# Sparse attention: three low parts on GpSimd, reordered joints, one place for u's high parts, gathered rows four columns later

## The chip, the cores and the metric

The kernel runs on one core of a Trainium2 chip. The metric is the time on the device in microseconds (us) of one execution of the whole program. An execution is also profiled; the profile gives the span from its first to its last instruction, and each engine's instructions. The engines are PE (TensorE, matmuls), DVE (VectorE), ACT (ScalarE), POOL (GpSimd) and SP (SyncE, which here only issues DMAs).

## The reference, cut to what matters

The input is 256 tokens of width 1024 in float32. There are two layers; each has an attention and then an expert network, and after each of the four comes `layer_norm(alpha * h + f(h))`.

- Layer 0's attention is latent attention with 16 heads.
- Layer 1's attention is sparse attention with 16 heads in 4 groups: per head a branch over compressed blocks, one over selected blocks and one over a window, each with a softmax, summed with learned gates. With 256 tokens the selected blocks and the window cover all earlier keys, so the last two branches run over the same causal pairs with keys and values of their own.
- The expert network: queries `h @ w_q` are scored against sub-keys, the 16 best of 128 x 128 experts are taken for each of 8 heads, and the result is the sum over the chosen experts e of `gate * gelu(u[e] . h) * v[e]`.

The kernel computes the expert network for nearly all tokens densely: u of all experts against all tokens, times a matrix of gates that is zero for experts not chosen, and then against all of v.

## The kernel before, in words

**Split matmuls.** All products are of float32 accuracy. Each weight tile (128 rows, 1024 columns) is split into a high part `hi`, which ACT rounds to the fast matmul type (line 125), and a low part `lo = raw - hi`, which DVE computes (line 136). Activations are split in the same way into `hT[0]` and `hT[1]`. A product is then three matmuls: high by high, high by low, low by high.

**The stream of weights.** All weight tiles of the program lie in one list, `stream`, in the order of use (`plan`, line 50). SP loads a tile into one of four places (`_sdma`, line 93), ACT makes its high part (`_shi`, line 113), DVE its low part (`_slo`, line 128), and PE uses both. `nxt` (line 154) hands out the next pair and prepares the ones after it: the low part of one tile and the high part of two tiles ahead. Four high and four low tiles exist at a time, so an engine runs at most a few tiles ahead of PE. `odd` says for a tile which of two offsets (0 or 32 elements) its high part has in its buffer: without an entry always 0, with one the offset alternates with the count `nh`. The four buffers lie 1056 elements apart, that is 16.5 times 64, so with the offset always 0 the tiles start by turns at two places modulo 64 elements, and with the alternating one all at the same place.

**Order.** Instructions run on each engine in the order in which the program writes them; there is no planner. What waits on an engine holds all that is written after it for that engine.

**The expert network** (`peer`, line 449) has a query stage, then 128 u steps (`u_step`, line 727: first narrow ones, and once the choice of experts is done wide ones, in which the high part meets both parts of the activations in one matmul of 512 columns), then 128 v columns (the loop that starts at `rate, gc`). A v column j takes one tile of v: ten matmuls, six for the first token half and four for the second. The 64 last tokens are not computed densely there. For them POOL gathers rows of v (`g_row`, line 476) and the activations of the chosen experts (`g_act`, line 482) by indirect DMA, and DVE multiplies and adds (`g_mac`, line 486, 64 times in column order). `LEAD` and `rate` set the columns in which this happens: gather c comes at column `LEAD + int(rate * c)`, and `rate` makes the last one fall on column 118. The last ten tiles of v are kept for the second token half ("kept tiles", `keep`).

**The joints.** After each attention or expert network comes a layer norm in two token halves (tt) and two column halves (hf): `ln_sum`, `ln_stats`, `ln_mid`, `ln_scale`, and `ln_T` (line 302), in which PE transposes, ACT copies the high part, and a returned function makes the low part on DVE. While the second token half is normalised PE starts on the next stage's first four weight tiles: `early_mm(tt, x, w, tiles)` (line 1229) runs the matmuls of token half tt with part x of the activations and part w of the weights; `early_close` (line 1241) runs all that are left. `ln_last` (line 321) writes out this order. It is called from the end of `peer` and from `out_close` (line 1152), the end of both attentions. Joint A is that after layer 0's attention, B that after layer 0's experts, C that after layer 1's attention.

**The sparse attention's head loop** (`for st in range(NH + 3)`, line 1501) runs one step per head: scores of head st, exponentials, the scaling of the probabilities of the head before (line 1566), transposes of the head two before, products with the values of the head three before. Beside it run, by step, the last two query tiles (steps 0 and 2), the compressed branch (steps 0 to 7, with small products on POOL), and from step 6 on every second step one tile of the output projection. `nxt` in these prepares weight tiles, and so low parts fall into steps 0, 2, 6, 8 and so on.

Of the kernel before, what the change touches and what calls it, by code (L numbers as in the profile page):

```python
# [34 lines left out]
FIRST, NEXT = 44, 10  # L35
GT = 64
ND = S - GT
RING, LEAD = 6, 7
AHEAD = 12
GB = 0.8  # L40
GS = 2.0 ** 15
# [2 lines left out]
class Kern:  # L44
# [5 lines left out]
    def plan(self):  # L50
        I, L = self.I, []
        self.v0s, self.spare, self.pairs = [], None, {}
        self.nh, self.odd = 0, {}
        if "mla" in self.parts:
            L += [I["a_w_in"][k] for k in range(KC)]
            L += [I["a_wk"][i] for i in range(2)]
            L += [I["a_wq"][i] for i in range(3)]
            L += [I["a_wv"][i] for i in range(2)]
            L += [I["a_wq"][i] for i in range(3, 6)]
            L += [I["a_wo"][i] for i in range(KC)]  # L60
        for l in (0, 1):
            if l == 1 and "nsa" in self.parts:
                L += [I["s_wv"][i] for i in range(4)]
                L += [I["s_wT"][i] for i in range(4)]
                L += [I["b_wg"]]
                L += [I["s_wT"][i] for i in range(4, 8)]
                L += [I["b_wq"][i] for i in range(4)]
                L += [I["b_wq"][i] for i in range(4, 8)]
                L += [I["b_wo"][i] for i in range(KC)] + [I["b_wo"][i] for i in range(KC // 2)]
            if f"peer{l}" in self.parts:  # L70
                L += [I["p_wq"][l, i] for i in range(16)]
                L += [I["p_u"][l, (P - FIRST + j) % P] for j in range(P)]
                self.v0s.append(len(L))
                o = (len(L) - self.v0s[0]) % 4
                self.odd.update((len(L) + j, 1) for j in range(P))
                self.pairs.update((len(L) + j, I["p_v"][l, j:j + 2].rearrange("j i d -> i j d")) for j in range(o % 2, P - 1, 2))
                L += [I["p_v"][l, j] for j in range(P)]
        self.stream = L
        self.v0 = self.vb = self.v0s[0]
        self.si = 0  # L80
        self.sd = 0
        self.sh = 0
        self.sl = 0
        self.raws, self.his, self.los = {}, {}, {}
        self.share = False
        self.alt = {}
        self.later, self.now = [], 0

# [39 lines left out]
    def _slo(self, upto, eng=None):  # L128
        while self.sl <= min(upto, len(self.stream) - 1):
            i = self.sl  # L130
            self._shi(i)
            raw = self.raws.pop(i)
            if i not in self.los:
                self.los[i] = self.shl.tile([P, raw.shape[-1]], F32R, tag="lo", name="lo")
            e = eng or (self.nc.gpsimd if self.share and i % 2 else self.nc.vector)
            e.tensor_tensor(self.los[i], raw, self.his[i].bitcast(F32), op=OP.subtract)  # L136
            self.sl += 1
            self._sdma(self._ahead())
# [182 lines left out]
    def ln_last(self, early, los=()):  # L321


        los, done = list(los), bool(los)
        if early:
            self.early_open()
            self.early_mm(0, 0, 0, (0, 1))
            self.early_mm(0, 1, 0, (0, 1))
        if not done:
            los.append(self.ln_T(0, 1))  # L330
        if early:
            self.early_mm(0, 0, 0, (2, 3))
        for hf in range(2):
            self.ln_scale(1, hf)
            if done and hf == 0:
                los.pop(0)()
            los.append(self.ln_T(1, hf))
            if done and early and hf == 0:
                self.early_mm(0, 1, 0, (2, 3))
            if early and hf == 0:  # L340
                self.early_mm(1, 0, 0, (0, 1))
        for f in los:
            f()
# [105 lines left out]
    def peer(self, l):  # L449
        tc, nc, I = self.tc, self.nc, self.I  # L450
        self.v0 = self.v0s.pop(0)
        with ExitStack() as es:
# [188 lines left out]
            done = {"g": 0, "a": 0}  # L641
# [154 lines left out]
            for j in range(P):  # L796
                x = u_step(j)
                u_fin(pu)
                pu = x
                g_flush(2)  # L800
                run_side(1.6 if len(A) == 1 else GB)
                if not side and len(A) == 1:
                    es_r.close()
                    if l == 1:
                        self.odd.update((i, 0) for i in range(self.si, self.v0))
                    hot = self.pr8.tile([P, 2, 3, 2, P, 2], F16, tag="r8", name="hot")
                    A.append((self.pr8.tile([P, NEXT, ND], F32, tag="r8", name="A2"), 0, NEXT))
                    n = P - FIRST - NEXT
                    A.append((pool(es_1, "slots1").tile([P, n, ND], F32, name="A1"), NEXT, n))
                    side.append(g_gen(hot))  # L810
                if done["g"] == ND and j >= P - 3 and not W:
                    w_start()
# [36 lines left out]
            def sum_1(f):  # L849

                t = self.ps()
                c, z = accs[1][f], hN[0:P - GT, 1, f * 512:(f + 1) * 512]
                nc.scalar.copy(t[0:P - GT], c[P - GT:P])
                nc.vector.scalar_tensor_tensor(z, z, ALPHA, c[0:P - GT], op0=OP.mult, op1=OP.add)
                nc.vector.tensor_tensor(z, z, t[0:P - GT], op=OP.add)
# [36 lines left out]
            early = l == 0 and "nsa" in self.parts  # L892
# [12 lines left out]
            lo0 = []  # L905
            for f in range(2):
                for j in range(P - NT, P - 3):
                    v_mm(j, 1, (f,), False, j == P - 4)
                    if f == 1 and j == P - 7:
                        lo0.append(self.ln_T(0, 1))  # L910
                sum_1(f)
                if early and f == 0:
                    self.lo_aside()
                self.ln_stats(1, f)
                if f == 0:
                    self.ln_T(0, 0)()
            self.ln_mid(1)
            self.ln_last(early, lo0)
        return hN


# [230 lines left out]
    def out_close(self):  # L1152
# [24 lines left out]
        early = "peer1" in self.parts if again else "peer0" in self.parts  # L1177
# [8 lines left out]
        for f in range(2):  # L1186
            self.out_mm(last[0], 1, (f,), False, False)
            self.out_mm(last[1], 1, (f,), False, True)
            self.ln_sum(1, f)
            if early and f == 0:  # L1190
                self.lo_aside()
            self.ln_stats(1, f)
            if f == 0:
                self.ln_T(0, 0)()
        self.ln_mid(1)
        self.ln_last(early)

    def heads_T(self, dst, h0, ps):

# [57 lines left out]
    def nsa(self, hN, gb):  # L1257
        tc, nc, I = self.tc, self.nc, self.I
# [3 lines left out]
        with es:  # L1262
# [237 lines left out]
            pr, pts = {}, {}  # L1500
            for st in range(NH + 3):
                self.tick()
                h = st
                if h < NH:
                    g = h // HG
# [169 lines left out]
```

## Time and profile before

| | us |
|---|---|
| three timed runs | 1750.76, 1750.95, 1747.94; median 1750.76 |
| the profiled execution | 1745.92 |
| its span | 1744.1 |
| PE busy | 1702.4 |
| DVE busy | 1553.4 |
| ACT busy | 1041.5 |
| POOL busy | 478.7 |

The mean granted clock of PE is 0.991 of full speed. Start times in the views are microseconds from the span's start. Matmuls are pipelined and their ends are modelled, so PE's busy time counts overlapping work once and a busy PE is not PE at its peak. "Idle before" is the time in which the engine stood still directly before an instruction; the arrow names what ended it.

### The profile page before, as it was taken

The numbers are of one execution on the slowest core, as the hardware profiler recorded it, in microseconds if no ns is written. First come the engines' busy times: TensorE is split into PE (matmuls) and PEld (weight loads), VectorE is DVE, ScalarE is ACT, GpSimd is POOL, SyncE is SP. The second block draws the span as 40 slices with busy tenths as digits, with TensorE's granted clock in tenths as the row PEclk, the third lists the DMA queues.
The fourth block names the chain that finished last, engine by engine and source line by source line (L and its number), as shares of the span: only waits on it lengthen the run. The fifth ranks groups of instructions, "written<-read, shape, count | busy, mean of one in ns | idle before, by whom it ended". The sixth has DMA issues, their size and how long they took to land.

```text
span 1744.1 us, 30698 instructions
## 1 busy us (share of the span) xinstructions
PE 1702.4 (98%) x10610; PEld 1480.5 (85%) x10610; DVE 1553.4 (89%) x3667; ACT 1041.5 (60%) x2265; POOL 478.7 (27%) x441
## 2 busy tenths in 40 slices
PE   7999999999999999999998999999999999999997
PEld 6779999888888788888786789998888888888886
DVE  6778988989997899999767789988999998999998
ACT  6656555766666455556455755556666666555554
POOL 2010002000002777761342210002000005777740
PEclk9999999999999999999998999999999999999999
DMA  7545667555557799999572265657556558999992
GB/s 245 174 145 180 203 192 266 184 183 185 183 184 259 301 395 373 368 358 328 176 246 90 84 215 179 204 182 270 187 182 188 183 183 297 401 383 369 361 363 108
DMA packets 118619, 416.66 MB, mean 239 GB/s; under 512 B 16032, under 2 KB 18112, under 8 KB 117376
## 3 DMA queue, kind: packets, MB, share of 16 engines
q1 hardware_dynamic: 88976, 322.60, 54.6%
q0 software_dynamic: 29488, 92.10, 14.2%
q8 instruction: 84, 1.38, 0.3%
q14 instruction: 71, 0.58, 0.1%
HBM read 400.49 MB, written 13.63 MB: 237 GB/s over the span
## 4 chain that ended last, share of the span: by engine, by line
PE 69%; issue 16%; DVE 7%; DMA 3%; ACT 2%; POOL 2%; SPq 0%; POOLq 0%; ACTq 0%; DVEq 0%
PE acc L202 36%; PE mm L202 33%; DVE lo L136 2%; PE mm L229 1%; DMA actD<-gst 1%; POOL row L479 1%; POOL actD L770 1%; DVE keep L136 1%; DMA raw<-a_wv 1%; ACT hi L125 0%; DMA xT<-xT 0%; DMA gel<-actD,gidx 0%; POOL gel L483 0%; DVE gacc L493 0%; DVE W L786 0%
## 5 line engine op out<-in xcount | busy, mean ns | idle before, releaser
L125 ACT CAST hi<-raw 128x1024 fp32r<-128x1024 f32 (+1 forms) x463 | 484.3, 1048 | 237.8 <-PE acc L202 96.7
L202 PE MATMUL mm<-hT,hi 128*128 128x256 f32 (+1 forms) x3360 | 610.7, 328 | 0.0
L136 DVE TENSOR_TENSOR lo<-raw,hi 128x1024 fp32r<-128x1024 f32 (+1 forms) x459 | 559.3, 1222 | 29.2 <-ACT hi L125 27.7
L202 PEld LDWEIGHTS mm<-hT,hi 128*128 128x128 f32 x3360 | 484.0, 188 | 44.0 <-issue 1.2
L202 PE MATMUL acc<-hi,W 128*128 128x512 f32 x1452 | 408.7, 390 | 0.0
L202 PEld LDWEIGHTS acc<-hi,W 128*128 128x128 f32 x1452 | 273.2, 188 | 56.9
L202 PE MATMUL mm<-hT,lo 128*128 128x256 f32 x2376 | 320.0, 277 | 0.0
L202 PEld LDWEIGHTS mm<-hT,lo 128*128 128x128 f32 x2376 | 306.9, 188 | 15.1
L202 PE MATMUL acc<-lo,W 128*128 128x512 f32 x968 | 299.6, 391 | 2.6 <-DVE lo L136 2.6
L770 POOL DMA_DIRECT2D actD<-gst x64 | 34.8, 544 | 785.0 <-ACT gst L768 785.0
L479 POOL DMA_INDIRECT row<-p_v,gidx x128 | 195.4, 1527 | 119.0 <-DVE gacc L493 81.7
L202 PEld LDWEIGHTS acc<-lo,W 128*128 128x128 f32 x968 | 181.6, 188 | 42.1 <-DVE lo L136 4.9
L125 ACT CAST hi<-spare 128x1024 fp32r<-128x1024 f32 x122 | 128.1, 1050 | 115.9 <-PE acc L202 99.8
L483 POOL DMA_INDIRECT gel<-actD,gidx x128 | 162.8, 1272 | 49.9 <-issue 36.0
L493 DVE SCALAR_TENSOR_TENSOR gacc<-row,ggate,gacc 128x1024 f32<-128x1024 f32 x126 | 161.3, 1280 | 1.1
L136 DVE TENSOR_TENSOR lo<-spare,hi 128x1024 fp32r<-128x1024 f32 x122 | 148.8, 1219 | 5.8 <-ACT hi L125 5.1
L762 ACT ACTIVATE mm<-mm 128x192 f32<-128x192 f32 (+23 forms) x170 | 40.9, 241 | 122.6 <-DVE mm L760 122.6
L786 DVE TENSOR_TENSOR W<-A,W 128x128 fp32r<-128x128 f32 (+1 forms) x512 | 107.5, 252 | 1.8 <-ACT W L781 1.8
L760 DVE TENSOR_TENSOR mm<-mm,half 128x256 f32<-128x256 f32 x174 | 74.5, 428 | 15.5 <-ACT half L759 14.9
L781 ACT CAST W<-A 128x192 fp32r<-128x192 f32 x256 | 88.2, 346 | 0.0
L659 DVE SCALAR_TENSOR_TENSOR A<-acc,A 128x176 f32<-128x176 f32 (+16 forms) x268 | 56.8, 274 | 24.9 <-PE acc L202 19.9
L765 ACT ACTIVATE A<-mm 128x192 f32<-128x192 f32 (+23 forms) x244 | 67.4, 276 | 7.2 <-DVE mm L760 2.2
(276 smaller groups left out, 1755.6 us busy)
## 6 DMA issues: line engine op xcount, KB each, us to landing
raw<-p_u SPq DMA_DIRECT2D x256, 512.0 KB, 3.8
spare<-p_v SPq DMA_DIRECT2D x64, 1024.0 KB, 8.9
raw<-p_v SPq DMA_DIRECT2D x63, 1024.0 KB, 8.9
raw<-p_wq SPq DMA_DIRECT2D x32, 512.0 KB, 4.0
actD<-gst POOLq DMA_DIRECT2D x64, 128.0 KB, 3.8
raw<-b_wo SPq DMA_DIRECT2D x12, 512.0 KB, 3.5
raw<-a_wo SPq DMA_DIRECT2D x8, 512.0 KB, 4.2
raw<-s_wT SPq DMA_DIRECT2D x8, 512.0 KB, 4.3
```

Of the source, the lines that this page charges most:

```text
L125: self.nc.scalar.copy(self.his[i], self.raws[i])
L136: e.tensor_tensor(self.los[i], raw, self.his[i].bitcast(F32), op=OP.subtract)
L202: self.nc.tensor.matmul(out, a, b, start=start, stop=stop)
L479: nc.gpsimd.indirect_dma_start(out=t, out_offset=None, in_=gtable, in_offset=bass.IndirectOffsetOnAxis(ap=gidx[:, 0, c:c + 1], axis=0))
L483: nc.gpsimd.indirect_dma_start(out=gel[c // 4][:, c % 4:c % 4 + 1], out_offset=None, in_=gplaces, in_offset=bass.IndirectOffsetOnAxis(ap=g ...
L493: nc.vector.scalar_tensor_tensor(gacc, t, gw[:, c:c + 1], gacc, op0=OP.mult, op1=OP.add)
L659: nc.vector.scalar_tensor_tensor(y, pv[:, j0:j0 + m], 1.0 / GS, y, op0=OP.mult, op1=OP.mult)
L760: nc.vector.tensor_tensor(ps[:, 0:S], ps[:, 0:S], t, op=OP.add)
L765: nc.scalar.activation(y[:, n:ND], ps[:, n:ND], AF.Gelu)
L770: nc.gpsimd.dma_start(self.actD[:, jj - 3:jj + 1, :], gst.pop())
L781: nc.scalar.copy(WW[j][:, 0:ND], slot(j))
L786: nc.vector.tensor_tensor(WW[j][:, o:o + c.stop - c.start], slot(j)[:, c], WW[j][:, c].bitcast(F32), op=OP.subtract)
```

## The change

Five edits:

1. `LEAD` goes from 7 to 11: gather c now comes at column 11 + int(1.703 c) instead of 7 + int(1.766 c).
2. An attribute `lo_eng` names the engine of low parts. It is DVE except in steps 0 to 7 of the sparse attention's head loop, where it is POOL.
3. `odd` gets its entries for the u tiles in both layers instead of layer 1 only, from the first tile without a high part.
4. The joints after the attentions: the low part of the first transposed quarter (tt 0, hf 0) is no longer made in the loop of the second half's sums but after `ln_scale(1, 0)`; the matmuls that need it move behind the transposes of (1, 0); two matmuls with the low part of the first weight tile are added before those transposes.
5. The joint after layer 0's experts: the low part of (0, 1) is made before the second half's sum instead of after `ln_scale(1, 0)`; its four matmuls move ahead of the transposes of (1, 0), with the two of the first weight tile's low part.

```diff
-RING, LEAD = 6, 7
+RING, LEAD = 6, 11
...
-        self.share = False
+        self.lo_eng = self.nc.vector
...
-            e = eng or (self.nc.gpsimd if self.share and i % 2 else self.nc.vector)
+            e = eng or self.lo_eng
...
     def ln_last(self, early, los=()):
-        los, done = list(los), bool(los)
+        los = list(los)
         if early:
             self.early_open()
             self.early_mm(0, 0, 0, (0, 1))
+        if los:
+            los.append(self.ln_T(0, 1))
+        elif early:
             self.early_mm(0, 1, 0, (0, 1))
-        if not done:
-            los.append(self.ln_T(0, 1))
         if early:
             self.early_mm(0, 0, 0, (2, 3))
+            if not los:
+                self.early_mm(0, 1, 0, (2, 3))
+            self.early_mm(0, 0, 1, (0,))
         for hf in range(2):
             self.ln_scale(1, hf)
-            if done and hf == 0:
+            if hf == 0 and los:
                 los.pop(0)()
             los.append(self.ln_T(1, hf))
-            if done and early and hf == 0:
-                self.early_mm(0, 1, 0, (2, 3))
             if early and hf == 0:
+                self.early_mm(0, 1, 0, (0, 1))
                 self.early_mm(1, 0, 0, (0, 1))
         for f in los:
             f()
...
-                    if l == 1:
-                        self.odd.update((i, 0) for i in range(self.si, self.v0))
+                    self.odd.update((i, 0) for i in range(self.sh, self.v0))
...
                     if f == 1 and j == P - 7:
                         lo0.append(self.ln_T(0, 1))
+                for x in lo0:
+                    x()
                 sum_1(f)
...
-            self.ln_last(early, lo0)
+            self.ln_last(early)
...
             if f == 0:
-                self.ln_T(0, 0)()
+                lo0 = self.ln_T(0, 0)
         self.ln_mid(1)
-        self.ln_last(early)
+        self.ln_last(early, [lo0])
...
             for st in range(NH + 3):
                 self.tick()
+                self.lo_eng = nc.gpsimd if st < 8 else nc.vector
```

## Rows read from the trace of the kernel before

**Rows 1.** The page of the whole execution, its part on engines: busy time, share of the span and number of instructions of each engine.

```profile
PE 1702.4 (98%) x10610; PEld 1480.5 (85%) x10610; DVE 1553.4 (89%) x3667; ACT 1041.5 (60%) x2265; POOL 478.7 (27%) x441
```

**Rows 2.** The chain of work that ended last, of the whole span: start, duration and what; the two long runs of narrow u steps, layer 0 and layer 1.

```profile
169.67 87.95 PE mm L202 x772
...
1065.92 87.95 PE mm L202 x772
```

**Rows 3.** The timeline of PE in the wide u steps and at the first matmul on v, in layer 0 (first two rows) and layer 1 (last two). Columns of a timeline: start, duration, engine, line, operation, what it writes and reads, number of instructions, and in brackets the idle time before them and what ended it.

```profile
352.81 2.02 PE L202 MATMUL mm<-hT,hi 128*128 128x512 f32 x8
...
547.56 0.62 PE L202 MATMUL acc<-hi,W 128*128 128x512 f32 x2
...
1245.87 2.00 PE L202 MATMUL mm<-hT,hi 128*128 128x512 f32 x8
...
1442.63 0.62 PE L202 MATMUL acc<-hi,W 128*128 128x512 f32 x2
```

**Rows 4.** The timeline at column 7 of layer 0's v stage (DVE, then PE), and PE's first matmuls on kept tiles in layer 0 and layer 1.

```profile
571.29 0.16 DVE L488 TENSOR_TENSOR ggate<-gel,ggate 128x4 f32<-128x4 f32 x1 [7.54 <-DMA gel<-actD,gidx]
...
573.47 1.22 PE L202 MATMUL acc<-lo,W 128*128 128x512 f32 x2 [2.58 <-DVE lo L136]
...
819.46 7.42 PE L202 MATMUL acc<-keep,W 128*128 128x512 f32 x32
...
1710.41 7.42 PE L202 MATMUL acc<-keep,W 128*128 128x512 f32 x32
```

**Rows 5.** Busy time by stretch, after PE's wait in layer 0's v stage and over layer 1's v stage. Columns: stretch, its length, busy us (and instructions) of PE, PEld (weight loads), DVE, ACT, POOL, granted PE clock, DMA share, GB/s.

```profile
573.40:577.00 3.60, 3.53 (x9) 2.85 (x10) 3.60 (x8) 0.57 (x1) 2.99 (x3) 0.54 0.02 0
...
1442.80:1700.00 257.20, 257.20 (x1135) 212.67 (x1135) 245.87 (x420) 148.84 (x233) 171.29 (x126) 1.00 0.98 368
```

**Rows 6.** The timeline of joint A: the low part of the first quarter on DVE, the sum behind it, PE's transposes of (1, 0).

```profile
113.67 0.67 DVE L313 TENSOR_TENSOR hT<-mm,hT 128x512 fp32r<-128x512 f32 x1
...
114.26 0.68 DVE L273 SCALAR_TENSOR_TENSOR hN<-hN,acc 128x512 f32<-128x512 f32 x1
...
118.40 0.63 PE L229 MATMUL mm<-ident,hN 128*128 128x128 f32 x4 [0.45 <-DVE hN L298]
```

**Rows 7.** The timeline of joint B: PE's early matmuls, the low part of (0, 1) on DVE, the transposes of (1, 0), those of (1, 1), and the closing block.

```profile
844.03 2.91 PE L202 MATMUL acc<-hi,hT 128*128 128x512 f32 x12
...
849.45 0.68 DVE L313 TENSOR_TENSOR hT<-mm,hT 128x512 fp32r<-128x512 f32 x1
...
849.58 0.97 PE L229 MATMUL mm<-ident,hN 128*128 128x128 f32 x4 [2.64 <-DVE hN L298]
...
853.52 0.60 PE L229 MATMUL mm<-ident,hN 128*128 128x128 f32 x4
...
854.79 3.02 PE L202 MATMUL acc<-hi,hT 128*128 128x512 f32 x12 [0.68 <-ACT hT L312]
```

**Rows 8.** Busy time by stretch, columns as in rows 5: joint B after its hole, and joint A.

```profile
850.00:853.40 3.40, 3.40 (x11) 2.75 (x10) 2.14 (x4) 0.58 (x1) 1.63 (x4) 0.53 0.53 128
...
112.00:121.00 9.00, 7.10 (x33) 4.68 (x32) 8.58 (x18) 2.58 (x5) 6.69 (x10) 1.00 0.43 146
```

**Rows 9.** The timeline of joint C: the last matmuls on the accumulator, and the second half's sum.

```profile
1008.53 1.64 PE L202 MATMUL acc<-keep,oT 128*128 128x512 f32 x6
...
1010.50 0.68 DVE L273 SCALAR_TENSOR_TENSOR hN<-hN,acc 128x512 f32<-128x512 f32 x1
```

**Rows 10.** The timeline of the sparse attention's head loop, steps 0 to 7: DVE's low parts of steps 2 and 6, PE's waits, and a product and the scalings beside them.

```profile
919.89 0.42 DVE L1458 TENSOR_TENSOR pc<-mm,mc 128x256 f32<-128x256 f32 x1 [1.02 <-PE mm L202]
...
929.19 1.22 DVE L136 TENSOR_TENSOR lo<-raw,hi 128x1024 fp32r<-128x1024 f32 x1
...
936.15 0.90 PE L229 MATMUL mm<-ident,p 128*128 128x128 f32 x3 [1.71 <-ACT pcT L1481]
...
947.06 0.73 POOL L1467 TENSOR_TENSOR pc<-pc,mc 128x256 f32<-128x256 f32 x1 [3.35 <-ACT pc L1466]
...
948.65 1.25 DVE L1566 TENSOR_SCALAR p<-p,m,gates 128x128 f32<-128x128 f32 x4
...
952.13 1.23 DVE L136 TENSOR_TENSOR lo<-raw,hi 128x1024 fp32r<-128x1024 f32 x1
...
955.22 0.44 PE L229 MATMUL mm<-ident,pc 128*128 128x128 f32 x2 [1.16 <-POOL pc L1475]
```

**Rows 11.** Busy time by stretch, columns as in rows 5, of steps 2 to 7 of that loop.

```profile
927.70:936.20 8.50, 4.69 (x27) 3.04 (x26) 7.33 (x23) 7.00 (x24) 0.62 (x1) 0.90 0.20 62
936.20:946.20 10.00, 10.00 (x52) 8.01 (x52) 7.57 (x20) 5.14 (x20) 2.98 (x3) 0.54 0.19 52
946.20:960.00 13.80, 11.09 (x74) 7.86 (x73) 11.17 (x32) 9.82 (x34) 1.35 (x2) 0.96 0.13 40
```

**Rows 12.** Line 136 on POOL, all low parts that it makes: number, shortest, median and longest duration in ns, first and last start.

```profile
L136 POOL TENSOR_TENSOR lo<-raw,hi x4: 2360/2394/2406, 27.7 to 1009.3; 128x1024 fp32r<-128x1024 f32 x4
```

**Rows 13.** The timeline where DVE and POOL work side by side: a low part beside a rotary product (before the loop), and scalings on both engines (step 9).

```profile
898.14 1.70 POOL L1214 TENSOR_TENSOR ropeO<-ropeU,ropeV 128x256 f32<-128x256 f32 x1
...
899.17 1.75 DVE L136 TENSOR_TENSOR lo<-raw,hi 128x1024 fp32r<-128x1024 f32 x1
...
967.29 0.67 DVE L1566 TENSOR_SCALAR p<-p,m,gates 128x128 f32<-128x128 f32 x2
...
967.48 2.14 POOL L1566 TENSOR_SCALAR p<-p,m,gates 128x128 f32<-128x128 f32 x2 [12.32 <-ACT pT L1529]
```

## The prediction

> **What bounds the kernel now.** I read the engine shares first: TensorE (PE) is busy 98% of the span, VectorE (DVE) 89%, GpSimd (POOL) 27% [rows 1]. So time can only come from three places: PE waiting, PE running at its lower clock, and PE doing the same work more slowly. I then read the chain that ended last for landmarks, and the timeline around each stage that the diff touches. The two expert layers run the same program: the narrow u steps of layer 1 start 1065.92 − 169.67 = 896.25 us after those of layer 0 and take the same 87.95 us [rows 2]. Layer 1 is therefore a control for layer 0, and any difference after that is the price of something that only layer 0 does.
>
> **The profiled execution and the median.** The rows come from an execution of 1745.92 us with a span of 1744.1 us; the three timed runs have a median of 1750.76 us (1747.94 to 1750.95). I work out the change on the span and take it off the median. A difference of 0.2%, 3.5 us, is about what a measurement of this kernel tells from none.
>
> **1. One place for u's high parts.** Layer 1's wide u steps alternate the offset of the high tiles already; layer 0's don't, so the edit changes layer 0 alone (in layer 1 only the first index of the range moves, over tiles already cast). In layer 0 a group of eight 512-column matmuls takes 2.02 us in every second step, in layer 1 it takes 2.00 [rows 3]. The first matmul on v comes at 547.56 and 1442.63, 895.07 us apart instead of 896.25 [rows 2, 3]: layer 0 loses 1.18 us. PE is the bound there, so I take all of it: **−1.2 us** (bounds 0 and −1.2).
>
> **2. The gathered rows start four columns later.** At column 7 of layer 0, DVE stands 7.54 us for the gathered activations. Queued behind that instruction is the low part of the next weight tile, and PE waits 2.58 us for it [rows 4]. For 3.6 us after that PE's granted clock is 0.54, mostly the 1.2 GHz level [rows 5]. From the first v matmul to the first one on kept tiles layer 0 takes 819.46 − 547.56 = 271.90 us, layer 1 1710.41 − 1442.63 = 267.78 [rows 3, 4]: both losses cost 4.12 us. A column is ten matmuls, 267.78 / 118 = 2.27 us, so four columns are 9.1 us, more than the 7.54 waited; DVE would arrive at 563.75 + 9.1 = 572.8, after the data at 571.29 [rows 4]. The wait goes in both layers; layer 1's never reached PE. **−4.1 us** (bounds −2.6, the wait alone, and −4.6).
> The cover: the same 64 multiply-adds now lie in 107 columns instead of 111. Even if all of DVE's work of layer 1's v stage were packed so, 245.87 × 4 / 107 = 9.2 us, it would fit into the 257.20 − 245.87 = 11.3 us in which DVE is idle there [rows 5]; so it costs nothing. The last gather stays at column 118. On POOL's queue the index gathers and row gathers move with their multiply-adds; the first twelve stay where they are.
>
> **3. The joints.** In both attention joints the low part of the first transposed half leaves its place ahead of the second half's sum. In joint A (layer 0's attention) it takes 0.67 us on DVE, and the sum starts only behind it, at 114.26 [rows 6]; the statistics and the second token half's scale follow in a row, so the transposes at 118.40 come 0.6 us earlier. The low part is made after that scale, behind which another centre and scale still follow, so the last transposes gain only 0.3. In PE's waits before and after these transposes there is now work: four matmuls with the low part, and two with the first weight tile's low part. The two are taken off the closing block, 2 × 0.227 = 0.45 us at the rate of a v column. Sum 0.3 + 0.45: **−0.8 us** for A. In joint C (layer 1's attention) the sum at 1010.50 stands behind the same work, but PE has the accumulator until 1008.53 + 1.64 = 1010.17 [rows 9], so the sum gains 0.3 instead of 0.6, and I take **−0.7 us**. Bounds for each: 0 and −1.4 (the whole 0.67 and more of the waits).
> Joint B (layer 0's experts) has the largest hole: twelve matmuls from 844.03, then PE waits 2.64 us for DVE until 849.58 [rows 7]. Six matmuls move into it, 1.36 us, leaving 1.3. The low part at 849.45 moves to a time when DVE is idle, so the last scale comes 0.6 us earlier. After the hole PE now runs at a granted clock of 0.53 [rows 8]. If the clock still falls, I put the closing block at 854.79 only 0.7 us earlier, about the last scale's gain, plus 0.45 for the two: −1.2. If it stays up, two rounds of transposes and copy (now 853.52 to 854.79, 1.27 us) and four matmuls (0.9) lie between 849.58 and the closing block, which then starts at 853.0 instead of 854.79 [rows 7]: −1.8, and with the two −2.2. Joint A keeps PE busy 7.10 of 9.00 us with several waits and its clock never falls [rows 8]. Hence I lean to the second: **−1.8 us**.
>
> **4. Three low parts to GpSimd.** Only the weight tiles prepared in steps 0, 2 and 6 move. DVE loses 1.22 us three times; POOL gains 2.39 each [rows 12]. The first saves nothing: DVE then waits 1.02 us for PE anyway [rows 10]. The second, at 929.19, stands ahead of the compressed branch's sums, the next maximum and the scaling that PE waits for; PE's wait of 1.71 us up to 936.15 ends at a copy at the end of that series [rows 10]. The third, at 952.13, stands ahead of the sums that POOL and then PE wait for, 1.16 us up to 955.22 [rows 10]. So the second and third give 1.14 each (a low part's step on DVE): **−2.3 us**. Queues: on POOL each stands ahead of a small product that its own sums release, and has run out before them; SP's next weight load goes out a little later in step 0, and none of these tiles is used before the next steps. Bounds: 0, if DVE loses as much beside POOL as it is spared (a low part of DVE's took 1.75 us instead of 1.22 beside a POOL product [rows 13]), and −5 with the clock rival below.
>
> **Sum**: 1.2 + 4.1 + 0.8 + 0.7 + 1.8 + 2.3 = 10.9 us; 1750.76 − 10.9 = **1740 us**.
>
> **Rivals.**
> *The clock stays up in the attention loop.* From 936.2 to 946.2 PE is busy all 10.0 us at a granted clock of 0.54 [rows 11], after waits that the change shortens by 1.1 us. Were it at 2.4 GHz, up to half would go; DVE and ACT then bind, so I price it at 3 us: 1737. Against it, the 1.71 us wait stays as long as it is, it only comes earlier. Chance 0.15.
> *POOL shuts DVE out.* While POOL works on a low part, DVE's scalings of the probabilities, from and to SBUF, would wait until it ends. In step 6 it follows POOL's product at 947.06 on that queue and runs to 947.06 + 0.73 + 2.39 = 950.2 [rows 10, 12]; the four scalings at 948.65 [rows 10] would wait 1.55 us, and with something like the half of it in step 2 part 4 gives nothing: 1742. Against it, DVE's two scalings at 967.29 took 0.67 us, as two of four do elsewhere, though POOL had begun at 967.48 [rows 10, 13]. Chance 0.12.
> The Trainium skill (SBUF — State Buffer, Who interferes with whom) states this rule: the port pair that DVE and GpSimd share is an exclusive lock for a whole instruction, and the loser blocks fully. By that rule this rival would be the forecast; the rows above show lengthening on both sides instead, and no scaling that was held.
> *The edits don't do what they say* in layer 0: another dependence holds DVE at column 11, or the offset isn't what slows PE. Parts 1 and 2 then fall to about 1 us: 1745. Against it, layer 1 as the control. Chance 0.08.
> *Slower than before.* PE's clock falls for the whole of steps 2 to 7, because the waits come closer together or DVE is held by POOL. Outside the stretch that is slow already PE is busy 4.69 + 11.09 = 15.8 us there [rows 11]; at 1.2 GHz these double: 1740 + 15.8 = 1755.6. It decides once more than 10.9 us of that work run at the lower level. Against it, the clock is 0.90 and 0.96 there now [rows 11]. Chance 0.03.
>
> **How the numbers follow.** The forecast with its own bounds (1736 to 1744) has 0.62. The range takes in the first three rivals and, since the timed runs differ among themselves by 3 us, a little more: 1733 to 1746. Forecast, clock, port and idle edits all end below 1747.3 (0.2% under the median), less a share of the worst combinations: faster 0.90, same 0.07, slower 0.03.
>
> **What would show it.** Part 1: u groups of 2.00 us in layer 0, and the first v matmuls of the layers as far apart as their narrow u steps. Part 2: no PE wait near column 7, equal v stages in both layers, no DVE wait on the activations. Part 3: the sum right behind the statistics in A and C; eighteen matmuls instead of twelve before the transposes in B, and the clock after them. Part 4: three more low parts on POOL of about 2.4 us, and DVE's scalings not longer than 0.31 us each. The prediction is wrong if layer 0's v stage stays 4 us longer than layer 1's, or if the attention loop as a whole gets longer.

## The result, and the profile after

The changed kernel takes **1738.73 us** (median of 5 runs, 1734.73 to 1741.48), the kernel before beside it 1748.84 us (5 runs, 1747.94 to 1750.95): ratio 0.9941, 95% interval 0.9926 to 0.9957. It is faster, and 1740 was forecast. The profiled execution of after took 1737.21 us (span 1735.4), 8.7 us less than that of before. PE's busy time fell by 3.5 us, and POOL's rose by 8.2, as against [rows 1]:

```profile
PE 1698.9 (98%) x10610; PEld 1478.6 (85%) x10610; DVE 1552.2 (89%) x3664; ACT 1041.9 (60%) x2265; POOL 486.9 (28%) x444
```

The two spans cut at landmarks of PE's timeline. A joint runs from its first transposes of `hN` to the next stage's first projection, the head loop from its first scores to its last products with the values.

| stage | before | after | difference | forecast |
|---|---|---|---|---|
| start to joint A | 111.25 | 110.42 | -0.83 | 0 |
| joint A | 17.27 | 16.36 | -0.91 | -0.8 |
| queries, layer 0 | 40.53 | 40.92 | +0.39 | 0 |
| u, layer 0 | 378.51 | 376.92 | -1.59 | -1.2 |
| v, layer 0, to the kept tiles | 271.90 | 267.70 | -4.20 | -4.1 |
| joint B | 21.41 | 22.19 | **+0.78** | **-1.8** |
| head loop | 79.98 | 78.89 | **-1.09** | **-2.3** |
| joint C | 16.60 | 15.99 | -0.61 | -0.7 |
| all the rest | 806.65 | 806.01 | -0.64 | 0 |

Four terms came as forecast in this execution; two did not, and some 1.1 us came from stages that the change doesn't touch. The experiments are about the two, and about which of these differences repeat.

Layer 0's expert network after, PE and DVE (start, duration, engine, line, operation, tiles, count), to be read against [rows 3, 4]:

```profile
350.60 2.00 PE L202 MATMUL mm<-hT,hi 128*128 128x512 f32 x8
...
544.62 0.62 PE L202 MATMUL acc<-hi,W 128*128 128x512 f32 x2
...
569.83 0.16 DVE L491 TENSOR_TENSOR ggate<-gel,ggate 128x4 f32<-128x4 f32 x1
...
812.32 7.41 PE L202 MATMUL acc<-keep,W 128*128 128x512 f32 x32
```

The u group takes 2.00 us, DVE's first product with the gathered activations has no idle time in front of it (7.54 us before), and 812.32 - 544.62 = 267.70 us is layer 1's time.

Joint A, PE's transposes of (1, 0), and the second half's sum on DVE, against [rows 6]:

```profile
112.85 0.67 DVE L273 SCALAR_TENSOR_TENSOR hN<-hN,acc 128x512 f32<-128x512 f32 x1
...
116.98 0.63 PE L229 MATMUL mm<-ident,hN 128*128 128x128 f32 x4
```

The sum stands right behind the statistics of the first half. From there to the transposes it is 4.13 us as before (118.40 - 114.26 = 4.14); all has moved up together.

Joint B, PE's timeline, then stretches of it (length, busy us and instructions of PE, PEld, DVE, ACT, POOL, granted PE clock, DMA share, GB/s), against [rows 7, 8]:

```profile
842.45 0.66 PE L229 MATMUL mm<-ident,hN 128*128 128x128 f32 x4 [1.28 <-DVE hN L298]
843.78 1.46 PE L202 MATMUL acc<-hi,hT 128*128 128x512 f32 x4 [0.67 <-ACT hT L312]
845.04 1.05 PE L229 MATMUL mm<-ident,hN 128*128 128x128 f32 x4
846.77 5.13 PE L202 MATMUL acc<-hi,hT 128*128 128x512 f32 x12 [0.68 <-ACT hT L312]
```

```profile
843.70:846.50 2.80, 2.31 (x8) 1.55 (x8) 0.75 (x2) 0.40 (x2) 0.79 (x2) 0.65 0.66 184
846.50:850.00 3.50, 3.23 (x8) 2.56 (x9) 3.25 (x4) 0.44 (x2) 0.00 (x0) 0.50 1.01 419
850.00:851.80 1.80, 1.80 (x7) 1.42 (x6) 0.84 (x1) 0.82 (x1) 0.00 (x0) 0.63 0.92 355
```

The hole shrank from 2.64 to 1.28 us, as worked out, and the closing block starts 8.02 us earlier than before, of which 7.14 came from the stages ahead. But the clock then falls to its 1.2 GHz level over the closing block, whose twelve matmuls take 5.13 us instead of 3.02; before, the fall lay over eight matmuls and was over when the block began.

The head loop, steps 1 and 5 to 6: DVE's maxima and the product m behind them (the row maximum times a constant, 4 elements per partition), POOL's low parts, PE's waits for the scaled probabilities:

```profile
919.77 2.37 POOL L136 TENSOR_TENSOR lo<-raw,hi 128x1024 fp32r<-128x1024 f32 x1
...
920.78 0.68 DVE L1556 TENSOR_REDUCE m<-acc 128x2 f32<-128x512 f32 x1
...
921.49 0.67 DVE L1557 TENSOR_SCALAR m<-m 128x4 f32<-128x4 f32 x1
...
923.35 0.99 PE L229 MATMUL mm<-ident,p 128*128 128x128 f32 x6 [2.15 <-DVE p L1573]
...
939.91 2.39 POOL L136 TENSOR_TENSOR lo<-raw,hi 128x1024 fp32r<-128x1024 f32 x1
...
940.34 1.98 DVE L1557 TENSOR_SCALAR m<-m 128x4 f32<-128x4 f32 x1
...
943.51 1.00 PE L229 MATMUL mm<-ident,p 128*128 128x128 f32 x6 [1.15 <-DVE p L1573]
```

The same product in step 5 of the kernel before:

```profile
948.36 0.17 DVE L1550 TENSOR_SCALAR m<-m 128x4 f32<-128x4 f32 x1
```

m takes 0.17 us in all 16 steps of the kernel before. Here it takes 0.67 and 1.98 us, and both times ends with POOL's low part (919.77 + 2.37 = 922.14, 939.91 + 2.39 = 942.30): it is held for 0.50 and 1.81 us. The maximum over a PSUM tile at 920.78 ran wholly within a low part and took its usual 0.68 us. So did, within the first of the three low parts (912.30 to 914.68), a maximum over an SBUF tile:

```profile
914.09 0.42 DVE L1466 TENSOR_REDUCE mcm<-pc 128x16 f32<-128x256 f32 x1
```

It takes 0.42 us in the kernel before too. PE's next transposes wait for the scalings behind m.

### The profile page after: what moved, and what is told of

The parts are those of the page before. It is cut to its first block, busy times and chain, and to the rows that moved or that the text cites. A ratio compares the mean times of both kernels' runs of the same rounds, so it can differ in the third digit from the quotient of the medians.

```text
span 1735.4 us, 30703 instructions
## 1 busy us (share of the span) xinstructions
PE 1698.9 (98%) x10610; PEld 1478.6 (85%) x10610; DVE 1552.2 (89%) x3664; ACT 1041.9 (60%) x2265; POOL 486.9 (28%) x444
## 4 chain that ended last, share of the span: by engine, by line
PE 91%; DVE 5%; ACT 2%; DMA 1%; issue 1%; POOL 0%; SPq 0%; ACTq 0%; DVEq 0%
PE mm L202 50%; PE acc L202 40%; PE mm L229 1%; DVE keep L136 1%; ACT hi L125 0%; DMA bounce<-ropeO 0%; DVE lo L136 0%; DVE gacc L496 0%; DMA raw<-p_wq 0%; DVE W L789 0%; DVE bnst L276 0%; ACT p L1563 0%; DVE m L1556 0%; DMA raw<-a_w_in 0%; ACT p L1560 0%
## 5 line engine op out<-in xcount | busy, mean ns | idle before, releaser
L482 POOL DMA_INDIRECT row<-p_v,gidx x128 | 187.5, 1465 | 116.6 <-DVE gacc L496 75.9
L486 POOL DMA_INDIRECT gel<-actD,gidx x128 | 171.9, 1343 | 49.8 <-issue 37.5
```

Source lines behind the costliest of these rows:

```text
L482: nc.gpsimd.indirect_dma_start(out=t, out_offset=None, in_=gtable, in_offset=bass.IndirectOffsetOnAxis(ap=gidx[:, 0, c:c + 1], axis=0))
L486: nc.gpsimd.indirect_dma_start(out=gel[c // 4][:, c % 4:c % 4 + 1], out_offset=None, in_=gplaces, in_offset=bass.IndirectOffsetOnAxis(ap=g ...
```

## The experiments

Each kernel was compared with the kernel before on the same chip. There the kernel before had medians of 1743.3 to 1744.8 us, not 1748.8; ratios are each against their own.

**The changed kernel once more**

> The changed kernel once more, to see which of its stage times repeat. If the stages read from its first trace are its own: from the first v matmul to the first one on kept tiles of layer 0 267.7 us; from the last two transposes of kept work in joint B to the next projection the joint costs 0.8 us more than before, with PE's granted clock near 0.5 for some 6 us behind the hole; in the head loop one small DVE instruction (m, line 1557) of about 2.0 us in step 6 and one of about 0.7 us in step 2, both ending with GpSimd's low part. If the joint's loss is chance, the clock stretch there is as short as before (3.6 us) and the joint gains 1 to 2 us. Time 1735 to 1742 us.

1737.71 us, ratio 0.9967 (0.9954 to 0.9979). Joint A 16.35, v 267.67, joint C 15.97 us repeat to 0.03. m of steps 1 and 5 (the expectations name the steps in which the low parts stand, 2 and 6) takes 0.69 and 1.82 us again. Not so joint B, 20.67 us, and the head loop, 79.42 at a mean granted clock of 0.89 instead of 78.89 at 0.94. The u stage took 378.58, of which 1.68 is one wait for DVE in the choice of experts (`hot`, line 636 of before); without it 376.9, as in the first trace. Over all traces this wait lay between 0 and 2.05 us, in the kernel before 0.66 and 0.44 us in its two layers: chance, not the change.

**Joint B as before**

```diff
-                for x in lo0:
-                    x()
                 sum_1(f)
...
-            self.ln_last(early)
+            self.ln_last_b(early, lo0)
```

`ln_last_b` is `ln_last` of the kernel before.

> The changed kernel with joint B (the end of layer 0's experts) in the order of before; the other four edits stay. Theory that the new order costs time through the clock: the joint is 0.8 us shorter than in the changed kernel (21.4 us from the transposes of the kept work, start of the first of the two groups, to the next projection, instead of 22.2) and the half-clock stretch 3.6 us instead of 6. Rival, that the lower clock falls there at random: the joint takes 22 to 23 us here too, or the changed kernel's repeat takes 20 to 21. By my forecast's step the old order would be 1.8 us longer.

1738.93 us, ratio 0.9970 (0.9960 to 0.9981). Joint B takes 21.52 us, with the fall of the clock where it was before:

```profile
842.85 0.72 PE L229 MATMUL mm<-ident,hN 128*128 128x128 f32 x4 [2.65 <-DVE hN L298]
843.45 3.61 PE L202 MATMUL acc<-hi,hT 128*128 128x512 f32 x8
...
848.18 3.01 PE L202 MATMUL acc<-hi,hT 128*128 128x512 f32 x12 [0.68 <-ACT hT L312]
```

With the old order it took 21.41, 21.52 and (in the kernel with the late rows alone) 21.14 us, each time with a fall. With the new order, and no filler, six executions of five kernels took 19.37 and 19.51 (granted clock 1.00), and 20.65, 20.67, 20.68 and 22.19 (with a fall). So neither theory holds as written: the order gains 0.85 us in the mean of these few (20.5 against 21.4), between a gain of 2.0 and a loss of 0.8, by whether the clock falls behind the hole, and on what.

**Filler in joint B's waits**

```diff
             self.early_mm(0, 0, 1, (0,))
+        fill = early and not los
+        if fill:
+            self.fill_mm(5)
...
             los.append(self.ln_T(1, hf))
+            if fill:
+                self.fill_mm((2, 2)[hf])
```

`fill_mm(n)` runs n matmuls of 512 columns into a PSUM tile that nobody reads.

> The changed kernel with nine matmuls more in joint B whose result nobody reads, in PE's waits: five before the transposes of (1, 0), two behind them, two behind those of (1, 1). Theory that PE's waits there bring the lower clock: the granted clock stays at 1.00 through the joint, the closing block's twelve matmuls take 3.0 instead of 5.1 us, and the next projection comes 2.5 to 3.5 us earlier after the same transposes. Rival, that the lower clock comes from something else (the DMAs, the weight loads, the run): the stretch stays and the joint gains nothing, or loses up to 1 us to the added matmuls.

1736.17 us, ratio 0.9966 (0.9954 to 0.9978). PE's timeline, and its clock from the hole on:

```profile
845.18 0.63 PE L229 MATMUL mm<-ident,hN 128*128 128x128 f32 x4 [0.20 <-DVE hN L298]
...
848.79 3.05 PE L202 MATMUL acc<-hi,hT 128*128 128x512 f32 x12 [0.21 <-ACT hT L312]
```

```profile
844.91:849.91 5.00, 4.39 (x22) 3.07 (x22) 3.34 (x6) 1.17 (x2) 2.24 (x5) 1.00 0.60 191
849.91:854.89 4.98, 4.98 (x23) 4.06 (x22) 4.09 (x4) 1.05 (x1) 0.00 (x0) 1.00 1.01 382
```

The clock stays up and the joint takes 19.48 us. So it did in all five kernels with this filler (19.45 to 19.48), against two of nine executions without it, old and new order together. PE's waits bring the fall there; the DMAs, as busy here as in the changed kernel (shares 0.60 and 1.01 against 0.66 and 1.01), don't.

**The low parts on GpSimd in four pieces**

```diff
-            e.tensor_tensor(self.los[i], raw, self.his[i].bitcast(F32), op=OP.subtract)
+            k = raw.shape[-1] // (4 if e is self.nc.gpsimd and eng is None else 1)
+            for c in range(0, raw.shape[-1], k):
+                e.tensor_tensor(self.los[i][:, c:c + k], raw[:, c:c + k], ...)
```

> The changed kernel with each of the three low parts on GpSimd in the head loop made in four pieces of 256 columns instead of one of 1024. Theory that a GpSimd instruction holds some of DVE's until it ends: the small instruction m of step 6 takes at most 0.8 us instead of 1.98, since it is held by one piece of 0.6 us only, though others behind it may be held as well; the head loop is 0.5 to 1.5 us shorter than in the changed kernel. Rival, that m waits for something else or that the two engines only share a rate: m stays near 2.0 us and the loop is not shorter.

1734.02 us, ratio 0.9951 (0.9939 to 0.9964). The loop takes 75.63 us at a mean clock of 0.98; with whole low parts and the same mean clock it took 77.04 us (the kernel with filler in joint B). DVE beside the third low part:

```profile
936.13 0.42 DVE L1560 TENSOR_SCALAR m<-m 128x4 f32<-128x4 f32 x1
936.46 0.17 DVE L1573 RECIPROCAL m<-m 128x4 f32<-128x4 f32 x1
936.66 2.38 DVE L1576 TENSOR_SCALAR p<-p,m,gates 128x128 f32<-128x128 f32 x4
```

```profile
935.79 2.85 POOL L138 TENSOR_TENSOR lo<-raw,hi 128x256 fp32r<-128x256 f32 x4
```

m is held for 0.25 us only, but the four scalings (1.25 us elsewhere) for 1.13: held by turns, one piece after the other, 1.4 us instead of 1.8. That is what the hold theory says; the rival, that m waits for something else or that the engines share a rate, had m near 2.0 us and the loop no shorter.

**m in another form**

```diff
-                    nc.vector.tensor_scalar(m[:, 1, :], m[:, 0, :], -scale, None, op0=OP.mult)
+                    nc.vector.tensor_tensor(m[:, 1, :], m[:, 0, :], neg, op=OP.mult)
```

`neg` is a new tile of 4 elements per partition, set to -scale ahead of the loop.

> The changed kernel with the small product m = max times -scale (line 1557, 4 elements) of the head loop written as a product of two tiles (TENSOR_TENSOR) instead of a tile with a constant (TENSOR_SCALAR). Theory that the form decides what GpSimd's low part holds: m then takes 0.2 us in step 6 and the reciprocal behind it 0.2, and the first of the four scalings of p (TENSOR_SCALAR) is held in its place, until the low part ends: the four take about 2.5 us instead of 1.25, and the loop is no shorter at the same clock. Rival, that whatever DVE does then is held: m still takes 1.8 to 2.1 us.

1754.41 us, ratio 1.0064 (1.0048 to 1.0079): 16 us slower than the changed kernel, which nobody expected. First the hold:

```profile
948.35 1.88 DVE L1559 TENSOR_TENSOR m<-m,neg 128x4 f32<-128x4 f32 x1
```

It stays, so the form does not decide; the theory as I wrote it falls. Then the time: the u stages take 385.08 and 385.93 us, nearly all of it PE work (385.06 and 385.69), in groups of 2.02 and 1.10 us where the changed kernel has 2.00 and 1.07:

```profile
320.21 2.02 PE L202 MATMUL mm<-hT,hi 128*128 128x512 f32 x8
322.07 1.10 PE L202 MATMUL mm<-hT,lo 128*128 128x256 f32 x8
```

**The same without a new tile**

```diff
+                    nc.vector.memset(m[:, 3, :], -scale)
-                    nc.vector.tensor_scalar(m[:, 1, :], m[:, 0, :], -scale, None, op0=OP.mult)
+                    nc.vector.tensor_tensor(m[:, 1, :], m[:, 0, :], m[:, 3, :], op=OP.mult)
```

> The kernel of r_mTT without its new tile of 16 bytes per partition: the constant -scale is written into a row of m that the reciprocal overwrites later (one short DVE instruction more in each of the 16 steps). Theory that the 16 us of r_mTT in the two u stages come from where the new tile moved the tiles behind it: groups of eight 512-column matmuls back to 2.00 us, PE work of a u stage 376.9 us instead of 385.1 and 385.7, 1736 to 1742 us as a whole. Rival, that they come from the changed instruction or the program around it: u stages of 385 us again. The hold of m, now TENSOR_TENSOR again, stays at 1.8 to 2.1 us in step 6.

1738.95 us, ratio 0.9963 (0.9945 to 0.9980); the u stages 377.06 and 377.21 us, groups of 2.00. The 16 bytes did it; that they did so by moving the tiles allocated behind them is the likely way, and was not looked at tile by tile. The hold is there again, and a memset beside the same low part isn't held:

```profile
937.96 2.39 POOL L136 TENSOR_TENSOR lo<-raw,hi 128x1024 fp32r<-128x1024 f32 x1
```

```profile
938.21 0.06 DVE L1557 MEMSET m<- 128x4 f32 x1
938.31 2.06 DVE L1558 TENSOR_TENSOR m<-m 128x4 f32<-128x4 f32 x1
```

**The low parts at other times**

```diff
+                if st in (0, 5):
+                    self.lo_behind(p[:, 0, 383:384] if st else m[:, 1, 0:1])
                 after()
```

Here `lo_behind` copies that column on GpSimd, which waits for it, and then makes the next low part there. The last two of the three low parts move in this way.

> The changed kernel with the last two of the three low parts on GpSimd made at other times: behind the small product m of step 0 and behind the scalings of step 5 (each through a copy of one column that waits for them). Theory that the forecast's saving is there and the holds took it back: no DVE instruction of the loop is held any more, m takes at most 0.3 us everywhere, PE's waits for p are 2.0 to 2.6 us in sum instead of 4.6 to 4.9, and the loop is 1.5 to 2.3 us shorter than in runs of the changed kernel with the same granted clock (at 0.98 about 75.0 us, at 0.89 about 77.5). Rival, that PE then waits for something else in the same chain (the exponentials on ACT, the transposes' copies): the holds go and the loop gains less than 0.7 us.

1736.57 us, ratio 0.9966 (0.9954 to 0.9978). m is no longer held, but the query's second split, which also works from SBUF to SBUF, is, for 1.5 us of its 2.81 (1.29 elsewhere). PE then waits 1.71 us for the small product behind it, where before it waited 1.16 [rows 10]:

```profile
939.85 2.37 POOL L136 TENSOR_TENSOR lo<-raw,hi 128x1024 fp32r<-128x1024 f32 x1
```

```profile
940.57 2.81 DVE L1382 TENSOR_TENSOR qs<-qr,qs 64x512 fp32r<-64x512 f32 x2 [0.92 <-ACT qs L1381]
```

```profile
945.35 0.44 PE L234 MATMUL mm<-ident,pc 128*128 128x128 f32 x2 [1.71 <-POOL pc L1485]
```

The loop took 76.88 us at 0.96, against 77.04 at 0.98 with the holds on m: the rival's case, nearly. The low part met the next DVE step of the kind that is held; other places were not tried.

**The two together**

> The kernel of r_shift with the nine matmuls of r_fillB in joint B. If both effects add: joint B 19.5 us at a granted clock of 1.00, the loop as in r_shift, 2 to 5 us faster than the changed kernel as a whole. If the joint's clock falls in spite of the filler, 20.7 to 22 us there.

1736.82 us, ratio 0.9967 (0.9955 to 0.9979). Joint B 19.47, as hoped; the loop, the same code that took 76.88 us, 80.76. Stretches of that loop here, up to the scores of step 8 and from there on:

```profile
905.02:949.60 44.58, 36.76 (x222) 29.04 (x223) 32.74 (x83) 26.20 (x86) 16.68 (x17) 0.81 0.29 97
949.60:985.78 36.18, 34.92 (x244) 25.12 (x244) 27.63 (x75) 29.08 (x102) 10.63 (x12) 0.95 0.23 73
```

PE is busy 71.7 us in it, where the same matmuls took 66.6 us in the kernel with the low parts at other times, and it does not wait longer: the lower clock makes the 4 us. Loops of different kernels can't be compared while it comes and goes.

**The late rows alone**

```diff
-RING, LEAD = 6, 7
+RING, LEAD = 6, 11
```

> The kernel before with the later gathered rows alone. By my forecast's step: layer 0's v stage up to the kept tiles 267.8 us instead of 271.9, no PE wait near column 11, DVE never waiting for the activations, 4.1 us faster as a whole; all other stages as before (joint A 17.3, joint B 21.4 if the lower clock behind its hole is no chance, joint C 16.6, u of layer 0 with 377.8 us of PE work). Rival, that the wait only moves to column 11: the stage takes 270 us or more. If joint B differs from 21.4 by over 0.7 us here, its clock is chance before the change too.

1742.11 us, ratio 0.9991 (0.9981 to 1.0002). The stage is as forecast, DVE does not wait for the activations, and PE's first matmuls on v and on kept tiles lie 267.51 us apart:

```profile
547.14 0.62 PE L202 MATMUL acc<-hi,W 128*128 128x512 f32 x2
...
814.65 1.52 PE L202 MATMUL acc<-keep,W 128*128 128x512 f32 x6
```

But as a whole it gained 1.9 us on that chip (at most 3.3 by the interval), not 4.1. The wait of 7.54 us is for a transfer; that it was shorter in the other executions of the kernel before is likely and was not seen, since only one of them was profiled. (The one profiled execution of each, 1745.92 and 1741.54 us, do differ by 4.4 us, as this stage does in them.)

**The head loop at a steady clock**

31 matmuls more in PE's waits of steps 0 to 4, on top of joint B's filler; then the same with all low parts on DVE, and with the pieces.

```diff
+                    fill({0: 6, 2: 5, 3: 4}.get(st, 0))
                     self.mm(s0v, q[:, 0:P], ks[:, g, :, 0:P], True, False)
...
+                        fill({(2, 0): 6, (3, 1): 6, (4, 0): 4}.get((st, br), 0))
                         for i in range(3):
                             self.tr(...)
```

> The kernel of r_fillB with 31 matmuls more, whose result nobody reads, in PE's waits of steps 0 to 4 of the head loop (6 before the scores of step 0, 5 and 4 before those of steps 2 and 3, 6, 6 and 4 before transposes of steps 2, 3 and 4). Theory that the loop's time in the changed kernel, 77.0 to 81.1 us with the same code, is set by where the lower clock falls, and that the waits bring it: the granted clock stays at 1.00 up to step 5 at least, the loop takes 76 to 77.5 us, joint B 19.5. Rival, that the clock falls whatever PE does: stretches at 0.5 as long as before, loop 79 us or more. If the added matmuls themselves cost, up to 2 us more than the 75.6 of the best loop so far.

> The kernel of f_pool with all low parts of the head loop on DVE, as before the change: the fourth part of the change alone, at what should be a steady clock in both. By my forecast's step the loop is 2.3 us longer than in f_pool. By the theory that GpSimd's low parts hold DVE for as long as they spare it (holds of 0.5 and 1.8 us against two low parts of 1.14 spared): within 0.6 us of f_pool, either way. If the clock falls in one of the two and not in the other, this decides nothing.

> The kernel of f_pool with GpSimd's low parts in four pieces. Held time falls from 2.3 us in sum to 1.9 us by the holds seen in the two traces: the loop is 0.3 to 0.6 us shorter than in f_pool. If r_pieces' loop of 75.6 us came from the pieces and not from the clock: 1.4 us shorter.

1735.67 us, ratio 0.9956 (0.9942 to 0.9970); all on DVE 1735.62, 0.9961 (0.9948 to 0.9975); pieces 1734.25, 0.9949 (0.9935 to 0.9962). The stretch from the first scores to those of step 8, in this order:

```profile
904.96:946.77 41.81, 36.63 (x247) 27.52 (x248) 33.26 (x83) 26.09 (x86) 16.15 (x15) 1.00 0.33 103
```

```profile
905.42:947.31 41.89, 37.04 (x247) 27.87 (x248) 34.48 (x87) 26.14 (x86) 9.11 (x12) 0.97 0.31 103
```

```profile
906.07:946.65 40.58, 36.14 (x247) 27.58 (x248) 32.91 (x83) 26.09 (x86) 17.45 (x24) 1.00 0.33 107
```

With the waits filled the clock stays up in these steps, and the first kernel's five timed runs lie within 0.8 us, those in pieces within 1.9 (the six of the changed kernel within 6.3; those with filler in joint B alone within 5.6; those with all low parts on DVE, whose clock falls from step 7 on, within 4.2). Between the first two lies part 4 of the change: **0.1 us**. With all low parts on DVE the last 2 us of the stretch were already at a lower clock; by my own condition a fall in one of the two decides nothing, but this one can only have lengthened the stretch of the kernel on DVE. So GpSimd's low parts gain 0.1 us or less here. In pieces they gain 1.2 us, more than the 0.3 to 0.6 expected: the held scalings then stand where DVE would wait 0.92 us for ACT anyway.

The same stretch without the 31 matmuls took 41.80 us (filler in joint B alone) and 41.84 (m without a new tile), both at a clock of 0.96, and 40.54 in pieces. So the matmuls cost nothing here, the pieces gain the same again, and the clock can stay near its upper level without filler, by chance. The whole loops took 77.81 (76 to 77.5 was expected), 78.53 and 75.70 us: in the first two the clock fell around step 8 all the same, behind the last filled wait.

The kernel in pieces and with filler has the ratio 0.9949, below the changed kernel's 0.9967 on the chips of the experiments, though the intervals overlap; the pieces without filler have 0.9951.

## Why the prediction was right, and where it wasn't

The time and its sign came as forecast, from terms of which two were wrong. That 10.1 us were measured where 10.9 were forecast is in part luck: in the repeat the same two kernels differed by 5.6 us, and the stages that repeat add up to 7.6 (below).

**Part 1** was right in kind. PE's work in layer 0's u stage falls from 377.83 us (377.68 in the kernel with the late rows alone) to 376.88, 0.95 us where 1.2 were forecast: 0.2 us of the difference between the layers that I took was the `hot` wait, which is chance. The 16-byte tile points the same way from another side: nothing but the places of tiles is known to have changed with it, and the rate did.

**Part 2** was right in the traced stage, -4.2 us against -4.1, with the cover as argued (no PE wait, equal stages). What fails is that one profiled execution stood for the kernel: timed alone the edit gave 1.9 us.

**Part 3**: joints A and C gave 0.9 and 0.6 us, against 0.8 and 0.7, in each kernel with their new order but the one with the 16-byte tile (0.8 and 0), and not in the kernel with the late rows alone (17.27 and 16.76 us). Joint B is the term that was mis-sized. "If the clock still falls, -1.2; if it stays up, -2.2" has the right cases: where it stayed up the joint took 19.4 us, 2.0 less. But I put the fall at its old length, behind the hole, where PE had little to do; it can come later and last longer, over the closing block, and then the joint loses 0.8. In the mean it gave 0.85 instead of 1.8.

**Part 4** is the step that failed. "The second and third give 1.14 each" came true, and was taken back by holds of 0.5 and 1.8 us on another instruction than the rival named: m and not the scalings. At a steady clock the sum is 0.1 us or less. My lower bound for this part (0, DVE loses beside POOL what it is spared) was the answer, and what the rival "POOL shuts DVE out" (0.12) says happened, to another instruction. I argued against it from [rows 13]: the low part of 1.75 us beside a POOL product was read as both engines slowing down. It can be read as a hold: the product ended at 898.14 + 1.70 = 899.84, and a low part of 1.22 that waits for it would end at 901.06; it ended at 900.92. And 967.29 is a DVE instruction that came first; POOL's two scalings beside it took 2.14 us, the next two, at 970.57, 1.22.

The Trainium skill (SBUF — State Buffer, Who interferes with whom) states an exclusive lock of the shared port pair between GpSimd and DVE operations in a two-port mode, or with two SBUF inputs where GpSimd's operation reads SBUF. The trace agrees: m was held as TENSOR_SCALAR (1.98 us) and as TENSOR_TENSOR of SBUF inputs (1.88, 2.06), the split and the scalings too, and maxima over PSUM (0.68) and SBUF (0.42) and a memset (0.06) were not. The prediction should have taken this rule as the forecast for part 4, at 0 and not -2.3.

The head loop's 1.09 us in the first trace was thus the clock: 77.0 to 81.1 us with the same code. The rival that the clock stays up was half right: it nearly does so in some executions (0.98 in the loops of 77.04 and 75.63 us), and it stayed at 1.00 up to step 8 in the two kernels with GpSimd's low parts whose waits were filled.

What stays open: the sum of the stages that repeat is 0.9 + 0.95 + 4.2 + 0.85 + 0.6 + 0.1 = 7.6 us, between the 10.1 us measured first and the 5.6 us of the repeat. Part 2's wait would account for it, if it differs between executions of the kernel before: with the 1.9 us that the edit gave alone instead of 4.2, the sum is 5.3. It fits that the kernel before was 4.1 to 5.6 us faster in the experiments than in the first measurement (1743.3 to 1744.8 against 1748.84) and the changed kernel only 1.0 us faster (1737.71 against 1738.73); no trace shows where those 4 to 5 us lie.

## What to carry to other kernels

Before an operation goes from DVE to GpSimd, look at what DVE does in those 2.4 us: here an element-wise DVE instruction with all its inputs in SBUF was held until GpSimd's ended, however short it was itself, and what was spared was lost again; maxima, a memset and a sum with one input in PSUM (0.42 us at 913.63, beside the first low part) were not held. Cut the operation into pieces, or put it where DVE does work of the second kind or waits anyway. Where PE waits 1 to 3 us between bursts, its clock can cost as much as the wait: price a joint with the fall on its most expensive block, and try unread matmuls in the waits, which here cost nothing that the traces show and in joint B always kept the clock up. One profiled execution gives the stage's price in that execution; a wait for a transfer in it may be chance, and another layer that runs the same program without the wait says so.

## What the hardware showed that I had not expected

- A DVE instruction on 4 elements per partition took 1.98 us instead of 0.17, until GpSimd's instruction of 2.39 us had ended; maxima over 256 and 512 elements beside such an instruction took their usual 0.42 and 0.68 us.
- A new tile of 16 bytes per partition made the u stages 8 and 9 us longer: groups of eight matmuls of 512 columns at 2.02 instead of 2.00 us, of 256 columns at 1.10 instead of 1.07, and the run of narrow u steps at 91.06 instead of 87.95.
- Nine more matmuls in joint B made it 1.2 us shorter than the same joint with one fall of the clock (19.48 against 20.67).
- The same head loop took 77.0 to 81.1 us by where the lower clock fell.
